# Sample rows of the expert layer summed on VectorE alone, and token rows spread over partitions by eight wide matmuls

## The chip, the cores and the metric

The kernel runs on one core of one Trainium2 chip. The metric is the device time of one execution in microseconds (us); a kernel's time is the median of its runs. PE (TensorE) does the matmuls, DVE (VectorE) and ACT (ScalarE) the elementwise work, POOL (GpSimd) issues gathers by index and some loads, SP (SyncE) issues the loads of the large tables.

## The reference

One inference step of a decoder with two layers, for 256 prompt tokens and 32 sample tokens of 1024 columns. Each layer ends in a mixture of 16384 experts, in which each token takes 8 x 16 = 128 experts by index:

```
def block(xb):
    ...
    top_s, pos = lax.top_k(cand, TOPK)
    expert = jnp.take_along_axis(cand_idx, pos, axis=-1)
    g = jax.nn.softmax(top_s, axis=-1).astype(xb.dtype)
    u = u_tab[expert]
    v = v_tab[expert]
    act = jax.nn.gelu(jnp.einsum('td,thkd->thk', xb, u), approximate=False)
    return jnp.einsum('thk,thkd->td', g * act, v)
```

The change is in how `xb` and the second einsum are brought about for the tokens whose `u` and `v` rows are gathered. All is float32.

## The kernel before

**The dense part.** 240 of the prompt tokens are done densely: both tables stream through the core, 128 tiles of 128 x 1024 each of `ut` and `vt` per layer, loaded on SP's queue. Each tile is split into a high part `wh` (ACT, L234) and a rest `wl` (DVE, L235). A `u` tile takes 24 matmuls of 240 columns (L463 to L465) into `pu`, and after every second one ACT stores its activation (L1340). A `v` tile takes 24 as well (`vmm`, L1317 to L1319) into `acc`; for every second one the stored activations, weighted meanwhile by the gates, are split into `gh` (ACT, L439) and `gl` (DVE, L440). This is the main stream.

**The gathered part.** The 16 prompt tokens that are left (`extra`, L1389) and the 32 sample tokens (`sample`, L1428) read their rows by index. A partition stands for a token and some of its heads, and one indirect DMA (`gather`, L1370, issued by POOL at L1372) brings one row of 1024 values for each of the 128 partitions into a tile `grow`: 16 such gathers from each table for `extra`, 32 for `sample`. In a first round DVE multiplies each gathered `u` row with the token's own row and sums it (L1410, L1455). The activation and the gate make of it one factor per partition and row (`act`, L1457 to L1460). In a second round the `v` rows are summed with these factors: `extra` does it on DVE into `saccx`, `sample` in two ways. The first `CPS[l]` rows, 8 in layer 0 and 4 in layer 1, are summed on TensorE: DVE makes `S2` (L1462), the product of all factors with the matrix `sel` that says which token a partition stands for, and two matmuls of 32 output columns per row (L1488) add up into a PSUM tile `so`, which ACT then copies out to `sacc[0]` (L1474). The rest is added up on DVE into `sacd`, one instruction per row (L1483 the first, L1481 the others). A gather is issued two rows ahead (`AH`); the tag `g4k` has 5 buffers in this part of the kernel, of which the two accumulators take one each and the rows three.

**What sets the order.** The main stream is written tile by tile. After each tile it calls `pump` (L1097), which lets generators in the background emit a step: those in `self.bg` by a budget of costs, and `self.bg2`, which is `extra` and then `sample`. While `v` tiles run and `self.bg` is empty, `bg2` makes one step per tile. A `yield` ends a step. Before the matmuls of L1488 `sample` sets `idle2` and waits until `self.bg` is nearly empty. Each engine works through its own list in the order of emission.

**Token rows.** For the products with the `u` rows each partition needs its token's row. `rows_in` (L1377) makes it from the transposed tokens `src`, which is 128 x 8 x 32: a matmul with the identity turns 128 x 32 columns around into 32 partitions of 128, and this is done four times for four groups of 32 partitions, 32 matmuls in all, into two PSUM tiles `hfp`, each copied by ACT to a half of `hft`. It is called once by `extra` and once by `sample` in each layer.

**The layer's end.** `peer_end` (L1493) first turns the sums back, with 24 matmuls into `pf`: for each of 8 column blocks one of `saccx`, one of `sacc[0]` and one of `sacd`, the last two added up in PSUM. VectorE's gates on `pf` follow.

## Time and profile before

| | us |
|---|---|
| median of 3 runs | 2097.3 (2096.06 to 2103.64) |
| profiled execution | 2090.24 |
| its span, first to last instruction | 2088.4 |
| PE busy in it | 1987.2 |
| DVE busy in it | 1690.8 |
| ACT busy in it | 915.4 |
| POOL busy in it | 360.5 |

The mean granted clock of TensorE is 0.985 of full speed. The busy shares are averages over the whole span, in which the stages differ, so the stages themselves are read from windows and timelines of the trace. Idle time of an engine is given with what ended it; "issue" there is time in which the engine waited for nothing that the profile shows. The main stream's pace can be read from the count of one of its lines in a stretch, 8 to a tile.

### The profile page before, as it was taken

Reading aid. Unit: us, or ns where it says so; the run is one execution under the profiler, and the core shown is the slowest. Engines: PE = TensorE matmul, PEld = TensorE weight load, DVE = VectorE, ACT = ScalarE, POOL = GpSimd, SP = SyncE. Lnnn points to the kernel's source line nnn. Section 1 sums busy time; section 2 is a strip of 40 time slices with the busy share of each in tenths; the row PEclk is TensorE's granted clock in tenths of the full one; section 3 lists DMA queues with packets and bytes.
Section 4 is the critical chain, followed back from the end, with each engine's and each line's share of the span. In section 5 each row is a group of like instructions: output and inputs, shape, how many; then the busy total and the mean of one; then the engine's idle time right before and its main releaser. Section 6 shows DMA issues by size and latency. Waiting matters only on the chain.

```text
span 2088.4 us, 46457 instructions
## 1 busy us (share of the span) xinstructions
PE 1987.2 (95%) x19170; PEld 1858.5 (89%) x19170; DVE 1690.8 (81%) x3392; ACT 915.4 (44%) x1215; POOL 360.5 (17%) x329
## 2 busy tenths in 40 slices
PE   7999999999999999999988889999999999999997
PEld 3777999999999999889966569999999999998997
DVE  3786898888889989777576478989888899887975
ACT  1855444444444444344341454444444444443443
POOL 1100001302211130253012200013031111302520
PEclk9999999999999999999999899999999999999998
DMA  9776456857867786799469734668578677956982
GB/s 366 256 258 225 129 184 192 311 173 247 297 210 251 244 300 218 263 330 339 141 193 258 271 130 131 191 198 305 166 268 279 222 240 244 318 171 227 339 303 72
DMA packets 135908, 493.88 MB, mean 236 GB/s; under 512 B 16032, under 2 KB 16544, under 8 KB 135056
## 3 DMA queue, kind: packets, MB, share of 16 engines
q1 hardware_dynamic: 93168, 334.09, 48.9%
q0 software_dynamic: 42528, 156.83, 21.2%
q8 instruction: 150, 2.46, 0.5%
q14 instruction: 62, 0.51, 0.1%
HBM read 483.41 MB, written 7.39 MB: 235 GB/s over the span
## 4 chain that ended last, share of the span: by engine, by line
PE 54%; issue 18%; DVE 12%; DMA 9%; POOL 4%; ACT 2%; SPq 0%; POOLq 0%; DVEq 0%; ACTq 0%
PE pu L465 7%; PE pu L463 7%; PE pu L464 7%; PE acc L1318 6%; PE acc L1317 6%; PE acc L1319 6%; DMA grow<-vt,ei 4%; POOL grow L1372 4%; DVE wl L235 3%; PE prj L463 2%; PE prj L465 2%; PE prj L464 2%; DMA R<-us 2%; PE adap L402 1%; PE pgt L1275 1%
## 5 line engine op out<-in xcount | busy, mean ns | idle before, releaser
L234 ACT CAST wh<-raw 128x1024 fp32r<-128x1024 f32 x583 | 610.6, 1049 | 609.5 <-PE acc L1318 327.7
L235 DVE TENSOR_TENSOR wl<-raw,wh 128x1024 fp32r<-128x1024 f32 x583 | 706.3, 1219 | 155.0 <-ACT wh L234 146.9
L465 PE MATMUL pu<-aH,wl 128*128 128x240 f32 x2048 | 566.0, 276 | 9.7 <-DVE wl L235 9.3
L1318 PE MATMUL acc<-gl,wh 128*128 128x240 f32 x2048 | 567.4, 277 | 6.3 <-DVE gl L440 6.2
L1317 PE MATMUL acc<-gh,wh 128*128 128x240 f32 x2048 | 570.1, 278 | 2.3 <-ACT gh L439 2.3
L463 PE MATMUL pu<-aH,wh 128*128 128x240 f32 x2048 | 567.3, 277 | 0.9 <-issue 0.7
L1319 PE MATMUL acc<-gh,wl 128*128 128x240 f32 x2048 | 566.5, 277 | 1.0 <-DVE wl L235 1.0
L464 PE MATMUL pu<-aL,wh 128*128 128x240 f32 x2048 | 563.6, 275 | 0.7 <-issue 0.7
L465 PEld LDWEIGHTS pu<-aH,wl 128*128 128x128 f32 x2048 | 389.5, 190 | 13.2 <-DVE wl L235 12.2
L1317 PEld LDWEIGHTS acc<-gh,wh 128*128 128x128 f32 x2048 | 391.0, 191 | 8.9 <-issue 4.6
L1318 PEld LDWEIGHTS acc<-gl,wh 128*128 128x128 f32 x2048 | 391.4, 191 | 8.5 <-DVE gl L440 8.3
L1319 PEld LDWEIGHTS acc<-gh,wl 128*128 128x128 f32 x2048 | 390.9, 191 | 1.7 <-DVE wl L235 1.6
L463 PEld LDWEIGHTS pu<-aH,wh 128*128 128x128 f32 x2048 | 388.5, 190 | 1.5 <-issue 1.3
L464 PEld LDWEIGHTS pu<-aL,wh 128*128 128x128 f32 x2048 | 388.8, 190 | 0.7 <-issue 0.7
L1340 ACT ACTIVATE store<-pu 128x480 f32<-128x480 f32 x128 | 73.2, 572 | 227.7 <-PE pu L465 227.6
L1372 POOL DMA_INDIRECT grow<-ur,ei x64 | 89.4, 1397 | 382.8 <-DVE grow L1455 275.2
L1372 POOL DMA_INDIRECT grow<-vt,ei x64 | 102.4, 1599 | 193.3 <-DVE grow L1455 113.2
L464 PE MATMUL prj<-aL,wh 128*128 128x288 f32 x392 | 116.3, 297 | 3.7 <-issue 3.7
L463 PE MATMUL prj<-aH,wh 128*128 128x288 f32 x392 | 119.6, 305 | 0.0
L1251 DVE TENSOR_TENSOR oA<-c,iT 128x1280 f16<-128x1280 f16 (+1 forms) x136 | 116.3, 855 | 0.0
L465 PE MATMUL prj<-aH,wl 128*128 128x288 f32 x392 | 116.1, 296 | 0.0
L1282 DVE SCALAR_TENSOR_TENSOR store<-pgt,store 128x460 f32<-128x460 f32 (+3 forms) x184 | 83.6, 499 | 33.2 <-PE pgt L1275 32.9
(366 smaller groups left out, 2681.4 us busy)
## 6 DMA issues: line engine op xcount, KB each, us to landing
raw<-ut SPq DMA_DIRECT2D x256, 512.0 KB
raw<-vt SPq DMA_DIRECT2D x256, 512.0 KB
adaw<-wada POOLq DMA_DIRECT2D x56, 512.0 KB
raw<-w SPq DMA_DIRECT2D x54, 512.0 KB
raw<-wq SPq DMA_DIRECT2D x32, 512.0 KB
adaw<-wada SPq DMA_DIRECT2D x18, 512.0 KB
R<-us POOLq DMA_DIRECT2D x32, 286.5 KB
store<-wada POOLq DMA_DIRECT2D x12, 512.0 KB
```

Source lines behind the costliest of these rows:

```text
L234: nc.scalar.copy(hf, r)
L235: nc.vector.tensor_sub(lf, r, hf.bitcast(F32))
L463: nc.tensor.matmul(pt, h[:, kb], ah[:, ka, n0:n1], start=f, stop=False)
L464: nc.tensor.matmul(pt, h[:, kb], al[:, ka, n0:n1], start=False, stop=False)
L465: nc.tensor.matmul(pt, lo[:, kb], ah[:, ka, n0:n1], start=False, stop=e)
L1251: v.tensor_tensor(a, self.iota2[:, None].to_broadcast([128, g, 128, 2]), bc(0, 128), op=ALU.is_equal)
L1282: v.scalar_tensor_tensor(sv, pg[:, :n, q0 - j0:q1 - j0].rearrange("p t j -> p j t"), 1.0 / 4096.0, sv, op0=ALU.mult, op1=ALU.mult)
L1317: nc.tensor.matmul(o, vh[:, d], wh, start=f, stop=False, skip_group_check=True)
L1318: nc.tensor.matmul(o, vh[:, d], wl, start=False, stop=False, skip_group_check=True)
L1319: nc.tensor.matmul(o, vl[:, d], wh, start=False, stop=e, skip_group_check=True)
L1340: nc.scalar.activation(store[:, s:s + 2], pu[:, :, :ND], AF.Gelu)
L1372: self.nc.gpsimd.indirect_dma_start(out=r, out_offset=None, in_=tab, in_offset=bass.IndirectOffsetOnAxis(ap=ei[:, w, c:c + 1], axis=0))
```

## The change

First, `sample` no longer uses TensorE for `v` rows. `CPS`, `S2`, the wait with `idle2`, the matmuls of L1488 and `sacc[0]` go; all 32 rows are added up on DVE into `sacd`, one per step. Second, `peer_end` has 16 matmuls in place of 24. Third, `rows_in` has ACT copy `src` four times side by side into `rep`, a buffer of the tag `g4k`, and eight matmuls of 128 columns take the place of 32 of 32 columns.

```diff
 def rows_in(self, src):
     nc, ps = self.nc, self.ps
+    rep = self.bp.tile([128, KT, 4, 32], F32, name="rep", tag="g4k", bufs=self.g4b)
+    nc.scalar.copy(rep, src[:, :, None, :].to_broadcast([128, KT, 4, 32]))
     hft = self.bp.tile([128, D], F32, name="hft", tag="g4k", bufs=self.g4b)
     for b in range(2):
         pt = ps.tile([128, 4, 128], F32, name="hfp", tag="g", bufs=2)
         for k in range(4):
-            for hg in range(4):
-                nc.tensor.matmul(pt[32 * hg:32 * hg + 32, k], src[:, 4 * b + k], self.ident,
-                                 start=True, stop=True, skip_group_check=True)
+            nc.tensor.matmul(pt[:, k], rep[:, 4 * b + k].rearrange("p a b -> p (a b)"), self.ident,
+                             start=True, stop=True, skip_group_check=True)
         nc.scalar.copy(hft[:, 512 * b:512 * b + 512], pt.rearrange("p a b -> p (a b)"))
...
 def sample(self, l, TKs):
...
     v.tensor_mul(act, act, g.rearrange("p h r -> p (h r)"))
-    S2 = self.bp.tile([128, 32, 32], F32, name="S2", tag="g4k", bufs=self.g4b)
-    v.tensor_mul(S2, act[:, :, None].to_broadcast([128, 32, 32]),
-                 self.sel[:, None, :].to_broadcast([128, 32, 32]))
-    yield 1200
-    self.idle2 = True
-    while len(self.bg) > 1:
-        yield 0
-    self.idle2 = False
-    po = ps.tile([128, 512], F32, name="so", tag="g", bufs=2)
+    yield 0
+    d = self.sacc = self.bp.tile([128, D], F32, name="sacd", tag="g4k", bufs=self.g4b)
     for c in range(32):
-        if c == CP:
-            self.sacc = [wp.tile([128, 512], F32, name="sacc", tag="sacc"),
-                         self.bp.tile([128, D], F32, name="sacd", tag="g4k", bufs=self.g4b)]
-            nc.scalar.copy(self.sacc[0], po)
         if c + AH < 32:
             gather(vrows, 1, c + AH)
         r = rows.pop((1, c))
-        if c >= CP:
-            d = self.sacc[1]
-            if c > CP:
-                v.scalar_tensor_tensor(d, r, act[:, c:c + 1], d, op0=ALU.mult, op1=ALU.add)
-            else:
-                v.tensor_scalar(d, r, act[:, c:c + 1], None, op0=ALU.mult)
-            yield 1200
-            continue
-        for i in range(2):
-            gq = 64 * (c % 2) + 32 * i
-            nc.tensor.matmul(po[gq:gq + 32], S2[:, c], r[:, 512 * i:512 * i + 512],
-                             start=c < 2, stop=c >= CP - 2, skip_group_check=True)
-        self.tp += 600
-        yield 0
+        if c:
+            v.scalar_tensor_tensor(d, r, act[:, c:c + 1], d, op0=ALU.mult, op1=ALU.add)
+        else:
+            v.tensor_scalar(d, r, act[:, c:c + 1], None, op0=ALU.mult)
+        yield 1200
...
 def peer_end(self, l):
...
-        nc.tensor.matmul(pf[:, k, XP:], self.sacc[0][:, 128 * (k % 4):128 * (k % 4) + 128],
-                         self.c32[:, 288 + 32 * (k // 4):320 + 32 * (k // 4)], start=True, stop=False,
-                         skip_group_check=True)
-        nc.tensor.matmul(pf[:, k, XP:], self.sacc[1][:, 128 * k:128 * k + 128], self.sel, start=False, stop=True,
+        nc.tensor.matmul(pf[:, k, XP:], self.sacc[:, 128 * k:128 * k + 128], self.sel, start=True, stop=True,
                          skip_group_check=True)
```

The lines after L99 move up by one in the changed kernel (L235 is L234 there). Three places show how the instructions stand.

VectorE in layer 0, where the round of `v` rows of the sample tokens begins; before, from the last step of the activation (L1460) on:

```order
L1460 TENSOR_TENSOR sact<-sact,gsel 128x32
L1462 TENSOR_TENSOR S_11427<-sact,c_68 128x1024
L235 TENSOR_TENSOR wl<-raw,wh 128x1024
L440 TENSOR_TENSOR gl<-store,gh 128x480
L235 TENSOR_TENSOR wl<-raw,wh 128x1024 x2
L440 TENSOR_TENSOR gl<-store,gh 128x480
L235 TENSOR_TENSOR wl<-raw,wh 128x1024 x2
L440 TENSOR_TENSOR gl<-store,gh 128x480
L1483 TENSOR_SCALAR sacd<-grow,sact 128x1024
L1481 SCALAR_TENSOR_TENSOR sacd<-grow,sact,sacd 128x1024
```

And in the changed kernel, from the same instruction on:

```order
L1459 TENSOR_TENSOR sact<-sact,gsel 128x32
L1469 TENSOR_SCALAR sacd<-grow,sact 128x1024
L234 TENSOR_TENSOR wl<-raw,wh 128x1024
L439 TENSOR_TENSOR gl<-store,gh 128x480
L1467 SCALAR_TENSOR_TENSOR sacd<-grow,sact,sacd 128x1024
L234 TENSOR_TENSOR wl<-raw,wh 128x1024
L1467 SCALAR_TENSOR_TENSOR sacd<-grow,sact,sacd 128x1024
L234 TENSOR_TENSOR wl<-raw,wh 128x1024
L439 TENSOR_TENSOR gl<-store,gh 128x480
L1467 SCALAR_TENSOR_TENSOR sacd<-grow,sact,sacd 128x1024
```

The instruction for `S2` is gone, and `sacd` begins one place after the activation instead of after eight instructions of the main stream; from there one accumulation stands in each tile until all 32 are done.

ScalarE at the first call of `rows_in` in layer 0, before:

```order
L1340 ACTIVATE store<-pu 128x480
L234 CAST wh<-raw 128x1024 x2
L1340 ACTIVATE store<-pu 128x480
L1386 COPY hft<-hfp 128x512 x2
L234 CAST wh<-raw 128x1024 x2
```

And in the changed kernel:

```order
L1339 ACTIVATE store<-pu 128x480
L233 CAST wh<-raw 128x1024 x2
L1339 ACTIVATE store<-pu 128x480
L1379 COPY rep<-hfx 128x1024
L1386 COPY hft<-hfp 128x512 x2
L233 CAST wh<-raw 128x1024 x2
```

The copy to `rep` stands behind the activation `store<-pu` of the tile just ended and before the two copies of `hfp`.

TensorE at the same call, before:

```order
L464 MATMUL pu<-aL,wh 128x240
L465 MATMUL pu<-aH,wl 128x240
L1384 MATMUL hfp<-c_68,hfx 32x128 x32
L463 MATMUL pu<-aH,wh 128x240
L464 MATMUL pu<-aL,wh 128x240
L465 MATMUL pu<-aH,wl 128x240
L463 MATMUL pu<-aH,wh 128x240
```

And in the changed kernel:

```order
L463 MATMUL pu<-aL,wh 128x240
L464 MATMUL pu<-aH,wl 128x240
L1384 MATMUL hfp<-c_68,rep 128x128 x8
L462 MATMUL pu<-aH,wh 128x240
L463 MATMUL pu<-aL,wh 128x240
L464 MATMUL pu<-aH,wl 128x240
L462 MATMUL pu<-aH,wh 128x240
```

The place in the main stream is the same; 32 matmuls that read `hfx` became 8 that read `rep`. On POOL the order of the gathers is the same in both kernels; six loads of `wada` that stand among the layer 0 gathers of `vt` come a few gathers earlier or later. In the changed kernel the last accumulation of `sample` stands four tiles later in layer 0 and two in layer 1.

## Rows read from the trace of the kernel before

**Rows 1.** The page's busy time of each engine (busy us, share of the span, instructions), its costliest groups of instructions for ScalarE and VectorE, and of the groups by line on VectorE two more; in a group's line stand the busy time, the mean ns of one, and the idle time before them with what ended it.

```profile
PE 1987.2 (95%) x19170; PEld 1858.5 (89%) x19170; DVE 1690.8 (81%) x3392; ACT 915.4 (44%) x1215; POOL 360.5 (17%) x329
L234 ACT CAST wh<-raw 128x1024 fp32r<-128x1024 f32 x583 | 610.6, 1049 | 609.5 <-PE acc L1318 327.7
L235 DVE TENSOR_TENSOR wl<-raw,wh 128x1024 fp32r<-128x1024 f32 x583 | 706.3, 1219 | 155.0 <-ACT wh L234 146.9
...
L440 DVE TENSOR_TENSOR gl<-store,gh 128x480 fp32r<-128x480 f32 x128 | 83.2, 650 | 0.0
L1481 DVE SCALAR_TENSOR_TENSOR sacd<-grow,sact,sacd 128x1024 f32<-128x1024 f32 x50 | 64.1, 1282 | 21.6 <-DMA grow<-vt,ei 20.7 <-DVE gl L440 0.3
```

**Rows 2.** Busy time in six stretches of the instructions of L1317 alone, the first of three matmuls of a `v` block (8 of them in a tile): the stretch in us, its length, PE busy (count), PEld busy (count), granted clock, DMA share, GB/s. The first three stretches lie in layer 0, the last three in layer 1.

```profile
876.93:897.88 20.95, 6.92 (x24) 4.55 (x24) 1.00 0.89 324
897.88:963.75 65.87, 49.52 (x177) 34.26 (x177) 0.97 0.97 363
980.00:1020.00 40.00, 32.63 (x120) 22.45 (x120) 1.00 0.70 213
1917.57:1927.55 9.98, 2.32 (x8) 1.52 (x8) 0.91 0.92 333
1927.55:2008.17 80.62, 62.36 (x225) 43.02 (x225) 0.99 0.96 348
2020.00:2056.00 36.00, 29.36 (x108) 20.22 (x108) 1.00 0.51 160
```

**Rows 3.** The same view of the first stretch of each layer, of the instructions of L1488 alone (the matmuls that sum sample rows).

```profile
876.93:897.88 20.95, 7.88 (x32) 1.15 (x32) 1.00 0.89 324
1917.57:1927.55 9.98, 4.59 (x16) 0.62 (x16) 0.91 0.92 333
```

**Rows 4.** The timeline of VectorE around the first and the last of the accumulations of sample rows in each layer: start us, duration us, engine, line, operation, out<-in, and in brackets the idle time before it with what ended it.

```profile
898.74 0.97 DVE L1483 TENSOR_SCALAR sacd<-grow,sact 128x1024 f32<-128x1024 f32 x1 [1.79 <-DMA grow<-vt,ei]
903.39 1.28 DVE L1481 SCALAR_TENSOR_TENSOR sacd<-grow,sact,sacd 128x1024 f32<-128x1024 f32 x1 [3.68 <-DMA grow<-vt,ei]
...
969.73 1.29 DVE L1481 SCALAR_TENSOR_TENSOR sacd<-grow,sact,sacd 128x1024 f32<-128x1024 f32 x1 [0.80 <-DMA grow<-vt,ei]
...
1927.67 0.75 DVE L1483 TENSOR_SCALAR sacd<-grow,sact 128x1024 f32<-128x1024 f32 x1 [2.71 <-PE so L1488]
1931.66 1.28 DVE L1481 SCALAR_TENSOR_TENSOR sacd<-grow,sact,sacd 128x1024 f32<-128x1024 f32 x1 [3.24 <-DMA grow<-vt,ei]
...
2008.03 1.28 DVE L1481 SCALAR_TENSOR_TENSOR sacd<-grow,sact,sacd 128x1024 f32<-128x1024 f32 x1
```

**Rows 5.** The timeline of GpSimd around the first gathers of `vt` rows of the sample tokens, four in layer 0 and the first of layer 1; columns as in rows 4.

```profile
869.29 1.71 POOL L1372 DMA_INDIRECT grow<-vt,ei  x1 [20.07 <-DVE grow L1455]
...
904.95 1.67 POOL L1372 DMA_INDIRECT grow<-vt,ei  x1 [4.04 <-DVE sacd L1481]
907.31 1.68 POOL L1372 DMA_INDIRECT grow<-vt,ei  x1 [0.69 <-DVE sacd L1481]
910.21 1.68 POOL L1372 DMA_INDIRECT grow<-vt,ei  x1 [1.22 <-DVE sacd L1481]
...
1909.93 1.68 POOL L1372 DMA_INDIRECT grow<-vt,ei  x1 [92.54 <-DVE grow L1455]
```

**Rows 6.** The view of one tile, `S` (which takes in `S2`): operation and count, duration of one in ns (least, median, greatest), first and last start in us.

```profile
L1462 DVE TENSOR_TENSOR S<-sact,c x2: 1225/1225/1225, 874.3 to 1914.9; 128x1024 f32<-128x1024 f32 x2
```

**Rows 7.** Busy time of each engine in a stretch of layer 0 in which row gathers and their products run beside the tiles: the stretch, its length, PE, PEld, DVE, ACT and POOL busy (count), granted clock, DMA share, GB/s.

```profile
520.00:540.00 20.00, 20.00 (x180) 20.00 (x179) 19.03 (x18) 9.24 (x11) 11.01 (x7) 1.00 1.01 394
```

**Rows 8.** The same view of the transposing back at the end of each layer, of the tile `pf` alone (PE, PEld and DVE busy).

```profile
1023.35:1029.38 6.03, 6.03 (x48) 5.89 (x48) 0.00 (x0) 0.89 0.61 183
2056.63:2061.91 5.28, 5.28 (x48) 5.28 (x48) 0.00 (x0) 1.00 0.01 3
```

**Rows 9.** The timeline of TensorE at the third call of `rows_in` (layer 1), the rows of `hfp`; columns as in rows 4, two records for one matmul of this shape.

```profile
1402.09 1.72 PE L1384 MATMUL hfp<-c,hfx 128*32 128x128 f32 x51
...
1403.99 0.44 PE L1384 MATMUL hfp<-c,hfx 128*32 128x128 f32 x5 [0.19 <-issue]
1404.73 0.44 PE L1384 MATMUL hfp<-c,hfx 128*32 128x128 f32 x6 [0.30 <-issue]
1405.49 0.38 PE L1384 MATMUL hfp<-c,hfx 128*32 128x128 f32 x2 [0.31 <-issue]
```

**Rows 10.** Busy time of the instructions of the tile `pu` (the main matmuls of a `u` tile) in four stretches, each from the start of a call of `rows_in`: PE, PEld and ACT busy (count). A matmul that already runs at the start of a stretch is counted in it.

```profile
361.62:371.34 9.72, 6.69 (x52) 6.13 (x51) 1.10 (x2) 1.00 0.83 286
1402.09:1416.22 14.13, 9.56 (x81) 9.24 (x81) 1.14 (x2) 1.00 0.84 287
595.12:598.69 3.57, 0.07 (x1) 0.00 (x0) 0.57 (x1) 1.00 0.95 291
1635.27:1638.83 3.56, 0.07 (x1) 0.00 (x0) 0.57 (x1) 1.00 0.78 260
```

**Rows 11.** The timelines of ScalarE and, in the last row, of VectorE at the first and the third call of `rows_in`; columns as in rows 4.

```profile
361.73 0.57 ACT L1340 ACTIVATE store<-pu 128x480 f32<-128x480 f32 x1 [1.75 <-PE pu L465]
...
368.29 0.59 ACT L1386 COPY hft<-hfp 128x512 f32<-128x512 f32 x1 [4.62 <-PE pu L465]
...
1408.62 0.58 ACT L1386 COPY hft<-hfp 128x512 f32<-128x512 f32 x1 [2.52 <-remote]
...
368.91 1.23 DVE L1410 SCALAR_TENSOR_TENSOR grow<-grow,hft 128x1024 f32<-128x1024 f32 x1 [6.68 <-ACT hft L1386]
```

More of the change, by code (lines that the diff above doesn't have):

```diff
@@ L98 @@
 BG4 = 1
-CPS = (8, 4)
 J1 = 46
@@ L1116, in pump @@
                 self.step2()
-                if self.bg2 is None or self.idle2:
+                if self.bg2 is None:
                     break
@@ L1228, in peer @@
         xtra = self.extra(l)
-        self.von = self.idle2 = False
+        self.von = False
         self.bg += [tk_sample(), fin(0), fin(1)]
@@ L1444, in sample @@
         rows = {}
-        CP = CPS[l]
         gather = self.gatherer(ei, rows)
```

## The prediction

> **What bounds the kernel now.** I read the page's busy shares first [rows 1]: TensorE is busy for 95% of the span, VectorE for 81%. So a VectorE instruction costs nothing by itself; it costs what it makes TensorE wait. The question for each stretch is how long TensorE takes per weight tile there. A tile of the second table (`v`) is 24 matmuls, 8 of them on L1317, so the count of L1317 in a window divided by 8 is the number of tiles done [rows 2]. Undisturbed, 40.00 us hold 120, and 36.00 us hold 108: 15 tiles and 13.5, both 2.667 us per tile. That is the floor that I measure everything against.
>
> The same rows show the stage that is changed, in layer 0 and in layer 1. While TensorE sums sample rows, 20.95 us hold 24 (3 tiles) and 9.98 us hold 8 (1 tile): 8.0 and 2.67 us of main work, so 12.95 and 7.31 us are lost to it. The group of the row matmuls [rows 3] has only 7.88 and 4.59 us of work in these stretches; the rest is TensorE standing still behind a matmul that waits for its gathered row, with the main matmuls queued behind it. Then VectorE sums the other rows: 65.87 us hold 177 (22.1 tiles, 2.98 us each), 80.62 us hold 225 (28.1 tiles, 2.87 us each). So a row on VectorE costs TensorE about 0.31 us in layer 0 and 0.20 us in layer 1, a row on TensorE 1.62 and 1.83 us.
>
> **Why a VectorE row costs anything.** Each tile needs one `wl` (1219 ns) and half a `gl` (650 ns), and the row adds 1282 ns [rows 1]: 2.83 us by these durations, slightly less as they follow each other with overlap, against 2.667 us of TensorE. VectorE is at its limit, and each wait of the row for its gather goes to `wl` behind it and on to TensorE. The rows themselves follow each other by (969.73 - 898.74) / 23 = 3.09 us in layer 0 and (2008.03 - 1927.67) / 27 = 2.98 us in layer 1 [rows 4]; a gather starts when VectorE has given a buffer back (904.95, 907.31, 910.21 [rows 5]).
>
> **Part 1: 12 more rows on VectorE, none on TensorE.** The order shows one row per tile from the tile after the activation, 32 tiles in a row. I compare 32 tiles from the start of the TensorE rows. Layer 0 before: 20.95 + 65.87 + (32 - 25.1) x 2.667 = 105.2 us; after, 32 x 2.98 = 95.4. Layer 1 before: 9.98 + 80.62 + (32 - 29.1) x 2.667 = 98.3; after, 32 x 2.87 = 91.8. The gain is 9.8 + 6.5 = **16.3 us**. The tile before the stage also loses the product for `S2` (1225 ns [rows 6]), whose cover was VectorE's slack, and ScalarE one copy; I cost them at nothing. Rows now end 4 tiles later in layer 0 and 2 in layer 1, with 17 tiles or more still to come, so the end isn't late. On the POOL queue six loads for the next layer's conditioning stand among the gathers, before as after; they are moved by a few gathers and have no one waiting near.
> Bounds: if rows dictate the pace at 3.09 and 2.98 us, the 32 tiles take 98.9 and 95.4, and the gain is 6.3 + 2.9 = 9.2. If the pace were the floor, 85.3 each, it is 19.9 + 13.0 = 32.9; a stretch with such rows and TensorE at full count does exist, 180 matmuls in 20 us at 394 GB/s [rows 7]. I take the pace that this stage itself showed, since there `gl` comes in every second tile.
>
> **Part 2: the transposing back at the layer's end.** Of 24 matmuls 8 go. The block takes 6.03 us in layer 0 and 5.28 in layer 1 [rows 8], TensorE does nothing else in it and VectorE waits for its end. A third of each: 2.0 + 1.8 = **3.8 us**. Bounds: 1.8 each, or 2.7 in all if the first write to a bank has a fixed part; 4.5 if VectorE's wait falls with it.
>
> **Part 3: spreading the token rows, four times.** Before: 32 small matmuls whose spread to 4 column groups lets them run together: 51 records, two for a matmul, in 1.72 us [rows 9]. But the burst doesn't end so. TensorE then issues in drops of 5 or 6 records, and what it loses is more than the array time. In the first call, 9.72 us hold 51 main matmuls, in the third (layer 1) 14.13 us hold 80 [rows 10]; at 0.111 us each (40.00 us / 360) 4.0 and 5.2 us are lost; in the second and fourth nothing but the burst is in 3.57 and 3.56 us. Together 16.4 us. In the first and third ScalarE gets its second half only at 368.29 and 1408.62, and VectorE stands for 6.68 us before the first row [rows 11].
> After: ScalarE makes a copy of 1024 columns first, and eight full matmuls wait for it. The copy stands behind the activation that itself waits for the matmuls just ahead, so nothing covers it: 0.57 us of activation, about 1.05 us for the copy (a cast of the same size takes 1049 ns [rows 1]), some 0.15 us of hand-over, then 8 x 0.22 us (5.28 / 24 [rows 8]) = 1.76. That is 3.53 us, four times 14.1 us: a gain of **2.3 us**, if 32 instructions in place of 128 go out without drops. VectorE's stand of 6.68 us should fall to about 3.7.
> Bounds: nothing hides the wait and the drops were an accident of the profile: the wait alone is added, 4 x 1.77 = 7.1 us lost. The wait is covered after all: 16.4 - 7.0 = 9.4 gained.
> The rows show four small matmuls in the time of about one large one: 51 records in 1.72 us are 67 ns a matmul, 0.27 us for four, against 0.22. The Trainium skill ("TensorE: Matmul & The Clock Gate", section "Part 3: Packing small matmuls — row/col tiling") has the same as a rule: matmuls on different column groups run in the array at once, so four narrow ones cost little more than one. By that rule alone the eight wide ones save no array time, this part loses 7.1 us for its copy, and the whole sum would be 13.0 instead of 22.4. The trace agrees with the rule on the burst and not on what comes after it.
>
> **Sum.** 16.3 + 3.8 + 2.3 = 22.4 us. The profiled execution took 2090.24 us, span 2088.4 and 1.8 around it; that becomes 2067.8. The median of the runs is 2097.3, 7.1 above; I carry the difference over: 2097.3 - 22.4 = **2074.9**. A measurement of this kernel can tell about 0.5%, 10.5 us, from no change.
>
> **Rivals.** (a) *Transfers bound the stage.* In the changed stretches the DMA engines are busy for 0.89, 0.97, 0.92 and 0.96 of the time [rows 2]. Four and two more tiles must be loaded in the same stage; if they fit only in the time left free, the gain of part 1 is 20.95 x 0.11 + 65.87 x 0.03 + 9.98 x 0.08 + 80.62 x 0.04 = 8.3 us, the sum 14.4, the time 2082.9. For it: 363 GB/s already. Against it: 394 GB/s seen [rows 7], and 32 rows, 32 tiles and 6 loads of 0.524 MB in 95.4 us are 385 GB/s, layer 1 without the loads 366.
> (b) *No change.* Part 1 at its low bound (9.2) and part 3 at its loss (7.1): 9.2 + 3.8 - 7.1 = 5.9, the time 2091.4.
> (c) *Slower: the gather's wait moves into VectorE's queue at its start.* The first rows now come while the gathers have just begun: the first started at 869.29 and 1909.93 us, and in the present kernel the first accumulations wait 3.68 and 3.24 us [rows 4, 5], with `wl` and the main stream behind. If such waits came at every third row, because three buffers go round, the pace would be 2.667 + 3.4 / 3 = 3.8 us, 32 tiles 121.6 us: 16.4 and 23.3 lost, less 6.1 elsewhere: 33.6 slower, 2130.9. It decides from a pace of 3.27 us on, where the sum is zero (203.5 us before, plus 6.1, over 64 tiles is 3.27). Against it: 24 and 28 rows in a chain already run at 2.98 and 2.87 with the same three buffers.
> (d) That the change isn't made: excluded, the order shows 32 accumulations in a layer and 8 matmuls for 32.
>
> **How the numbers follow.** The forecast 0.62, (a) 0.17, (b) 0.14, (c) 0.07. The forecast's own range goes from 2063 (part 1 about 8 better than its pace, part 3 a few better) to 2085. (a) lies in it, (b) reaches to 2091.4; leaving out (c) and the far ends gives **2062 to 2091**. Faster by over 0.5% (under 2086.8): the forecast and (a), 0.79, less a little for their edges, 0.78; same: 0.15; slower: 0.07.
>
> **What would show it.** Right: no stretch where TensorE does 3 tiles in 20 us; L1317's successor at 8 per 2.9 us over 32 tiles; a dip of the granted clock (0.91 in the 9.98 us) gone; the block at the layer's end at 4.0 and 3.5 us; after each copy a TensorE wait of 1.6 to 1.9 us and then 16 records without gaps. Wrong: rows 3.3 us apart with VectorE waiting for gathers; waits for `wl` in place of the matmuls' waits; drops after the eight matmuls as before.

## The result, and the profile after

The changed kernel takes 2072.1 us (median of 4 runs, 2067.63 to 2073.99) against 2096.7 (2093.36 to 2103.64): a ratio of 0.9879, with an interval of 0.9853 to 0.9904, that is 1.2% faster. Its profiled execution took 2067.63 us, span 2065.8, 22.6 us less than the one before. The forecast was 2074.9, with 22.4 us gained, in a range from 2062 to 2091. The time was right, in part by luck: the runs below show that two of the three terms of the sum were not, and that for the largest, whose size was about right, the reason given was not.

First the page and the groups by line, to be held against [rows 1]:

```profile
PE 1962.2 (95%) x18898; PEld 1844.5 (89%) x18898; DVE 1702.2 (82%) x3402; ACT 919.3 (44%) x1217; POOL 367.6 (18%) x329
L234 DVE TENSOR_TENSOR wl<-raw,wh 128x1024 fp32r<-128x1024 f32 x583 | 707.7, 1222 | 126.5 <-ACT wh L233 121.4
...
L1467 DVE SCALAR_TENSOR_TENSOR sacd<-grow,sact,sacd 128x1024 f32<-128x1024 f32 x62 | 79.5, 1283 | 24.9 <-DMA grow<-vt,ei 24.5
```

VectorE has 11 us more to do and waits less for `wh` (121 us in place of 147). The stage is best read in windows that run from the start of the same tile to the start of another. Here of the kernel before and then of the changed one, the main matmuls of one line alone (PE and PEld busy with counts, granted clock, DMA share, GB/s): 33 tiles of layer 0 and 38 of layer 1 that hold all the `v` rows of the sample tokens, and two of the last three `v` tiles with the transposing back between them, in layer 0 and in layer 1.

```profile
874.13:982.94 108.81, 73.76 (x265) 50.75 (x265) 0.98 0.94 350
1906.61:2021.61 115.00, 84.29 (x305) 58.09 (x305) 0.99 0.92 330
1020.67:1034.44 13.77, 5.65 (x16) 4.27 (x17) 0.77 0.39 119
2053.95:2066.30 12.35, 5.24 (x16) 3.85 (x17) 0.86 0.01 1
```

```profile
878.76:980.90 102.14, 72.62 (x265) 50.04 (x265) 1.00 0.96 366
1894.43:2002.37 107.94, 83.64 (x304) 57.65 (x305) 1.00 0.96 349
1018.63:1027.59 8.96, 4.49 (x16) 3.04 (x17) 1.00 0.56 186
2034.71:2043.67 8.96, 4.49 (x16) 3.04 (x17) 1.00 0.01 2
```

The stage went from 108.81 to 102.14 and from 115.00 to 107.94 us. What it would be without rows is in the changed kernel's 14 tiles just behind it, 2.695 us each:

```profile
980.90:1018.63 37.73, 30.76 (x112) 21.20 (x113) 1.00 0.70 219
```

So 33 tiles have a floor of 88.9 and 38 one of 102.4, and the changed kernel is still 13.2 and 5.5 us above it. The layer's end went from 13.77 to 8.96 and from 12.35 to 8.96, more than the block itself, whose two windows of the tile `pf` answer to [rows 8]:

```profile
1021.32:1024.81 3.49, 3.49 (x32) 3.49 (x32) 0.00 (x0) 1.00 0.53 174
2037.50:2041.00 3.50, 3.50 (x32) 3.44 (x31) 0.00 (x0) 1.00 0.02 5
```

The rest is the clock. The tile that follows the block in layer 0, before and after (same columns as above):

```profile
1029.19:1034.44 5.25, 3.45 (x8) 2.79 (x9) 0.50 0.01 4
```

```profile
1024.81:1027.59 2.78, 2.29 (x8) 1.59 (x9) 1.00 0.52 183
```

Before, TensorE had the lower of its two levels there (0.50, 1.2 GHz in place of 2.4) after 24 matmuls of 16 and 32 columns in a row; the same work took 5.25 us in place of 2.78. After 16 such matmuls it kept 2.4 GHz in this trace, in both layers.

The first and the last accumulation of sample rows in each layer (timeline of VectorE, to be held against [rows 4]):

```profile
879.07 0.76 DVE L1469 TENSOR_SCALAR sacd<-grow,sact 128x1024 f32<-128x1024 f32 x1 [0.18 <-DMA grow<-vt,ei]
...
977.94 1.28 DVE L1467 SCALAR_TENSOR_TENSOR sacd<-grow,sact,sacd 128x1024 f32<-128x1024 f32 x1
...
1902.98 0.97 DVE L1469 TENSOR_SCALAR sacd<-grow,sact 128x1024 f32<-128x1024 f32 x1 [0.26 <-DMA grow<-vt,ei]
...
1994.03 1.28 DVE L1467 SCALAR_TENSOR_TENSOR sacd<-grow,sact,sacd 128x1024 f32<-128x1024 f32 x1
```

They begin without the waits of 3.68 and 3.24 us that the first ones had, and run (977.94 - 879.07) / 31 = 3.19 and (1994.03 - 1902.98) / 31 = 2.94 us apart.

At the first call of `rows_in`, ScalarE, TensorE and VectorE in the changed kernel (timelines; to be held against [rows 9, 11]):

```profile
362.90 0.57 ACT L1339 ACTIVATE store<-pu 128x480 f32<-128x480 f32 x1 [1.75 <-PE pu L464]
363.37 1.04 ACT L1379 COPY rep<-hfx 128x1024 f32<-128x1024 f32 x1
```

```profile
364.46 2.05 PE L1384 MATMUL hfp<-c,rep 128*128 128x128 f32 x16 [1.59 <-ACT rep L1379]
```

```profile
370.05 1.23 DVE L1410 SCALAR_TENSOR_TENSOR grow<-grow,hft 128x1024 f32<-128x1024 f32 x1 [6.43 <-DMA grow<-ur,xi]
```

TensorE waits 1.59 us for the copy, and its 16 records go out without drops: that is as forecast, in all four calls. But VectorE waits 6.43 us as before (6.68), now for the first gathered row instead of for `hft` (5.72 us in the third call).

### The profile page after: what moved, and what is told of

It reads as the page before. It is cut to its first block, busy times and chain, and to the rows that moved or that the text cites. A ratio compares the mean times of both kernels' runs of the same rounds, so it can differ in the third digit from the quotient of the medians.

```text
span 2065.8 us, 45941 instructions
## 1 busy us (share of the span) xinstructions
PE 1962.2 (95%) x18898; PEld 1844.5 (89%) x18898; DVE 1702.2 (82%) x3402; ACT 919.3 (44%) x1217; POOL 367.6 (18%) x329
## 4 chain that ended last, share of the span: by engine, by line
PE 54%; issue 18%; DVE 13%; DMA 8%; POOL 4%; ACT 3%; DVEq 0%; SPq 0%; POOLq 0%; ACTq 0%
PE acc L1317 7%; PE acc L1316 7%; PE acc L1318 7%; PE pu L464 5%; PE pu L462 5%; PE pu L463 5%; DMA grow<-vt,ei 4%; POOL grow L1371 4%; DVE wl L234 3%; PE prj L462 2%; PE prj L464 2%; PE prj L463 2%; PE adap L401 1%; DMA R<-us 1%; PE pd L881 1%
## 5 line engine op out<-in xcount | busy, mean ns | idle before, releaser
L234 DVE TENSOR_TENSOR wl<-raw,wh 128x1024 fp32r<-128x1024 f32 x583 | 707.7, 1222 | 126.5 <-ACT wh L233 121.4
L1317 PE MATMUL acc<-gl,wh 128*128 128x240 f32 x2048 | 566.3, 277 | 9.5 <-DVE gl L439 9.2
L1316 PE MATMUL acc<-gh,wh 128*128 128x240 f32 x2048 | 566.9, 277 | 2.3 <-ACT gh L438 2.3
L462 PE MATMUL pu<-aH,wh 128*128 128x240 f32 x2048 | 566.5, 277 | 0.0
L463 PE MATMUL pu<-aL,wh 128*128 128x240 f32 x2048 | 562.9, 275 | 0.0
L1317 PEld LDWEIGHTS acc<-gl,wh 128*128 128x128 f32 x2048 | 388.9, 190 | 13.6 <-DVE gl L439 12.9
L464 PEld LDWEIGHTS pu<-aH,wl 128*128 128x128 f32 x2048 | 389.1, 190 | 12.2 <-DVE wl L234 12.0
L1316 PEld LDWEIGHTS acc<-gh,wh 128*128 128x128 f32 x2048 | 388.5, 190 | 2.7 <-ACT gh L438 2.7
L463 PEld LDWEIGHTS pu<-aL,wh 128*128 128x128 f32 x2048 | 388.0, 189 | 0.0
L462 PEld LDWEIGHTS pu<-aH,wh 128*128 128x128 f32 x2048 | 387.1, 189 | 0.4 <-issue 0.4
L1371 POOL DMA_INDIRECT grow<-ur,ei x64 | 89.4, 1397 | 382.5 <-DVE grow L1454 268.7
L1371 POOL DMA_INDIRECT grow<-vt,ei x64 | 109.0, 1703 | 189.2 <-DVE grow L1454 111.9
L462 PE MATMUL prj<-aH,wh 128*128 128x288 f32 x392 | 119.5, 305 | 0.0
L463 PE MATMUL prj<-aL,wh 128*128 128x288 f32 x392 | 116.1, 296 | 0.0
```

Of the source, the lines that this page charges most:

```text
L234: nc.vector.tensor_sub(lf, r, hf.bitcast(F32))
L462: nc.tensor.matmul(pt, h[:, kb], ah[:, ka, n0:n1], start=f, stop=False)
L463: nc.tensor.matmul(pt, h[:, kb], al[:, ka, n0:n1], start=False, stop=False)
L464: nc.tensor.matmul(pt, lo[:, kb], ah[:, ka, n0:n1], start=False, stop=e)
L1316: nc.tensor.matmul(o, vh[:, d], wh, start=f, stop=False, skip_group_check=True)
L1317: nc.tensor.matmul(o, vh[:, d], wl, start=False, stop=False, skip_group_check=True)
```

## The experiments

Times are medians; a ratio is to the kernel before on the same chip. "Stage" means the windows above, 33 tiles of layer 0 and 38 of layer 1; "end" the windows of the last tiles.

| run | us (before) | ratio, interval | stage 0 | stage 1 | end 0 | end 1 |
|---|---|---|---|---|---|---|
| kernel before | 2096.7 | | 108.8 | 115.0 | 13.8 | 12.4 |
| changed | 2072.1 (2096.7) | 0.9879, 0.9853 to 0.9904 | 102.1 | 107.9 | 9.0 | 9.0 |
| e1 | 2098.5 (2095.3) | 1.0020, 1.0002 to 1.0038 | 114.7 | 113.3 | 12.4 | 14.0 |
| e2 | 2078.5 (2095.3) | 0.9929, 0.9902 to 0.9956 | 101.7 | 109.9 | 9.0 | 10.6 |
| e3 | 2074.3 (2095.3) | 0.9904, 0.9876 to 0.9931 | 100.4 | 108.8 | 12.4 | 14.0 |
| e4 | 2070.8 (2095.3) | 0.9889, 0.9864 to 0.9913 | 103.7 | 109.1 | 10.6 | 9.0 |
| e5 | 2053.8 (2094.6) | 0.9804, 0.9779 to 0.9830 | 89.0 | 102.5 | 9.0 | 10.5 |
| e6 | one run, 2056.4 | | 89.0 | 102.5 | 10.6 | 10.6 |
| e7 | one run, 2064.9 | | 97.8 | 107.4 | 12.2 | 12.0 |
| e8 | 2107.6 (2094.6) | 1.0075, 1.0046 to 1.0104 | 120.5 | 118.0 | 15.3 | 14.0 |
| e10 | 2044.8 (2093.2) | 0.9752, 0.9729 to 0.9774 | 89.4 | 102.5 | 10.6 | 12.0 |
| e11 | one run, 2055.9 | | 91.4 | 102.5 | 10.5 | 11.8 |
| e12 | 2041.6 (2093.2) | 0.9738, 0.9712 to 0.9764 | 91.3 | 102.5 | 9.0 | 9.0 |
| e13 | 2036.8 (2089.8) | 0.9734, 0.9708 to 0.9761 | 89.0 | 102.5 | 9.0 | 9.0 |

**e1: part 3 alone.** The kernel before with the new `rows_in`.

> The kernel before with part 3 alone: the copy to rep and eight wide matmuls in each of the four calls, sample rows and layer's end as before. My theory from the two traces: a call costs TensorE 1.59 us of waiting for the copy and 1.81 us for the matmuls, 3.40 us where the old burst took 3.57 in the second and fourth call, so those gain 0.2 each; in the first and third call the old loss is replaced by the wait for the first gathered row behind which wl stands, so they gain 0 to 1. Together 0 to 2.5 us faster than the kernel before, not to be told from it. Rival one, the prediction's part 3 as written: 2.3 faster. Rival two, the narrow matmuls were free and the copy is pure loss: 7.1 us slower.

It is 0.2% slower, with an interval of 0.4 to 8 us that just leaves out no change, and with it my theory and rival one; rival two's 7.1 us lie in it. But the calls themselves show no loss: 12 tiles around the first took 38.7 us in place of 38.5, around the third 37.8 in place of 38.7, and four around the second and the fourth 15.4 in place of 15.5. Its profiled execution took 2090.31 us, as long as the one before (2090.24); layer 0's stage, which the edit doesn't touch, is 5.9 us longer in it, and other places are shorter. So the traces have no place for a loss of 7 us in the calls, and none for a gain; the medians alone don't exclude the loss.

**e2: parts 1 and 2 alone.** The changed kernel with the old `rows_in`.

> The changed kernel with the old way of spreading token rows (32 narrow matmuls, no copy): parts 1 and 2 without part 3. My theory: nearly the whole gain stays, 22 to 25 us faster than the kernel before. Rival (the copy loses 7.1 us in the changed kernel): 31 us faster than the kernel before, that is 7 faster than the changed one.

The ratio gives 15 us of gain (9 to 21), less than my theory and the rival had. That would leave part 3 some 10 in the changed kernel, where e1 has a small loss for it. The two don't add up, and the traces have no place for either: the first call cost 1.5 us more in the changed kernel's profile, the third 0.8 less. It is not only the occasion: e3 and e4, measured beside e2, have the new `rows_in` and are 4 and 8 us faster than e2 by the medians. In the windows of the calls part 3 is about nothing; what it is worth in the medians stays open.

**e3: part 2 undone.** A third tile is turned back beside the two sums:

```diff
+        self.s0 = wp.tile([128, 4, 128], F32, name="sacc", tag="sacc")
+        nc.scalar.mul(self.s0, self.ones[:, None, :].to_broadcast([128, 4, 128]), 0.0)
...
+            nc.tensor.matmul(pf[:, k, XP:], self.s0[:, k % 4], ..., start=True, stop=False, ...)
-            nc.tensor.matmul(pf[:, k, XP:], self.sacc[:, 128 * k:128 * k + 128], self.sel, start=True, stop=True,
+            nc.tensor.matmul(pf[:, k, XP:], self.sacc[:, 128 * k:128 * k + 128], self.sel, start=False, stop=True,
```

> The changed kernel with 24 matmuls at the layer's end again: a third tile that holds zeros is turned back beside the two sums, so part 2 alone is undone. Theory A (the block of small matmuls and the waits around it bring TensorE to its lower clock, which the tile behind then pays for): 6 to 9 us slower than the changed kernel, that is 16 to 19 faster than the kernel before, and the granted clock at 0.5 in or right behind the block in one or both layers, with the last two tiles 5 us in place of 2.8. Rival (only the block's own length counts): 2.3 + 1.8 = 3.5 to 4.5 us slower than the changed kernel, clock 1.00 at both blocks.

The ends of the two layers, in the window of the changed kernel's 8.96 us:

```profile
1015.63:1027.98 12.35, 5.18 (x16) 3.82 (x17) 0.86 0.41 135
2040.76:2054.74 13.98, 5.66 (x16) 4.25 (x17) 0.76 0.00 1
```

Both are back at 12 to 14 us, with clocks of 0.86 and 0.76. At full clock they would be 12.35 x 0.86 and 13.98 x 0.76, 10.6 us each: 1.7 us are the block's length and the rest is the clock. Theory A holds in the trace, where the two ends are 8.4 us longer than the changed kernel's; the medians (21 us faster than before, 15 to 26) can't tell it from the changed kernel's 25 (20 to 31). Over all kernels here the end took 13.5 us on average with 24 matmuls (8 layer ends, a fall of the clock at each) and 10.1 with 16 (20 ends, a fall at 11 of them). TensorE stands still at none of these 28 ends, so of theory A's two reasons the block is left and the waits around it are not. So the 16 matmuls make a fall rarer and don't exclude it; that the changed kernel's profile has none at either end is partly chance.

**e4: the copy earlier.** `rep` is made when `bg2` is set up, for `sample` before its `yield 400`; `rep_in` holds the two lines that made it:

```diff
+                self.repx = self.rep_in(self.hfx)
                 self.bg2 = chain(xtra, smp)
...
+        rep = self.rep_in(self.hfs)
         yield 400
-        hft = self.rows_in(self.hfs)
+        hft = self.rows_in(rep)
```

> The changed kernel with rep copied earlier: for the extra tokens two tiles earlier, for the sample tokens one tile earlier; all else the same. Theory A (in the first and third call the first gathered row is late anyway, VectorE and the wl behind it wait for it, so only the second and fourth call gain): 2 x 1.59 = 3.2 us faster than the changed kernel. Rival B (TensorE's wait for the copy is lost time in each call): 4 x 1.59 = 6.4 us faster. Rival C (something else holds TensorE at these places): no gain.

What the instructions of `hfp` waited for (us, times, PE and PEld together), in the changed kernel and then in e4:

```profile
  ACT rep L1379: 13.5, 8
```

```profile
  PE hfp L1388: 2.5, 8
```

The second is the only wait left there, ScalarE's for the matmuls: TensorE's wait for the copy is gone in all four calls. The 12 tiles around the first and the third call took 40.4 and 38.3 us, 40.2 and 37.9 in the changed kernel: no gain there. For the second and fourth call the 3.2 us are too small for the medians, but the traces show them: the four tiles around each took 13.56 us in place of 15.43, 1.9 less twice. So theory A holds in the traces, and rivals B and C fall.

**e5: two rows in three tiles.**

```diff
+            self.td = max(self.td, self.tp)
             yield 1200
+            while self.pn % 3 == 2:
+                self.td = max(self.td, self.tp)
+                yield 0
```

> The changed kernel with the 32 rows of the sample tokens accumulated in two of three tiles instead of in each, over 47 tiles instead of 32; work and transfers are the same. In the changed kernel the stage of rows costs TensorE 0.43 us per tile above its floor in layer 0 (102.1 us for 33 tiles from the 79th v tile on, floor 88.0) and 0.17 us in layer 1 (107.9 us for 38 tiles, floor 101.3). Theory A (VectorE has no slack in a tile with a row, 2.83 us against 2.667, so every wait for a gather reaches TensorE): with 2.40 us of VectorE work per tile the waits are covered and most of the 14.1 + 6.6 us comes back, 12 to 20 us faster than the changed kernel. Rival B (transfers bound the stage): the same bytes over 47 tiles in place of 32, so some 10 us come back in layer 0 and little in layer 1. Rival C (each row's wait for its gather reaches TensorE whatever VectorE's load): no gain, within 3 us.

```profile
880.68:969.63 88.95, 72.52 (x264) 49.96 (x265) 1.00 0.98 368
1889.95:1992.45 102.50, 83.59 (x304) 57.63 (x305) 1.00 0.90 323
```

The stage is at its floor in both layers (L1316 alone), with 33 and 38 tiles in 88.95 and 102.50 us, and the kernel is 41 us faster than the one before. The rows now run on past these windows, and the tiles behind lose nothing either: the 14 behind layer 0's window took 37.73 us, as in the changed kernel. Rival C falls. Whether VectorE or the transfers got the room, the next two tell.

**e6: half the gathers, all of VectorE's work.** Every second gather is left out and each row used twice.

> The changed kernel with every second gather of vt rows for the sample tokens left out: each gathered row is accumulated twice, with two factors, so half of the sum's rows are wrong. VectorE's work is unchanged, the stage's gathers are halved. Theory A (VectorE is at its limit and the gathers' waits come on top): the pace falls to VectorE's own 2.83 us, 33 tiles of layer 0 in 93 to 95 us where the changed kernel has 102.1, 38 tiles of layer 1 in 105 to 107 where it has 107.9. Rival B (transfers bound): both fall to the floor, 88 to 89 and 101 to 102 us. Rival C (VectorE's work alone sets it): no change, within 1 us of 102.1 and 107.9.

Busy time of all engines in the two stages (PE, PEld, DVE, ACT, POOL), and in the second fence all that VectorE waited for these gathers in layer 0 (us, times, longest):

```profile
878.27:967.22 88.95, 88.95 (x795) 88.95 (x793) 85.77 (x84) 43.11 (x50) 25.94 (x20) 1.00 0.92 333
1887.74:1990.24 102.50, 102.50 (x920) 102.50 (x916) 97.52 (x98) 48.57 (x57) 27.37 (x17) 1.00 0.81 289
```

```profile
DVE sacd L1470 <- DMA grow<-vt,ei: 0.2, 1, 0.2
```

With one full row per tile and VectorE busy for 85.77 of 88.95 us, TensorE is at its floor. Theory A's VectorE at its limit falls: it needs 2.60 us per tile (85.77 / 33) of 2.695. The changed kernel's own stage in layer 0 says the same, with as much VectorE work in a longer time:

```profile
878.76:980.90 102.14, 92.98 (x795) 90.09 (x793) 85.47 (x83) 43.09 (x50) 55.83 (x37) 1.00 0.96 366
```

What B forecast came.

**e7: all gathers, hardly any work on VectorE.**

```diff
-                v.scalar_tensor_tensor(d, r, act[:, c:c + 1], d, op0=ALU.mult, op1=ALU.add)
+                v.scalar_tensor_tensor(d[:, :64], r[:, :64], act[:, c:c + 1], d[:, :64], op0=ALU.mult, op1=ALU.add)
```

> The changed kernel with the accumulations of the sample tokens' vt rows made on 64 of 1024 columns only, so most of the sum is left out; all gathers are issued and waited for. Theory A (a full VectorE passes the gathers' waits on): VectorE has 1.1 us of slack in each tile and takes the waits up, 33 tiles of layer 0 in 88 to 92 us, 38 of layer 1 in 101 to 103. Rival B (transfers bound): no change in layer 0, 100 to 104 us. Rival C (waits for gathers reach TensorE whatever VectorE's load): 96 to 102 us in layer 0.

```profile
877.29:975.13 97.84, 91.80 (x795) 89.72 (x794) 56.40 (x84) 43.04 (x50) 49.89 (x37) 1.00 0.98 379
1889.99:1997.36 107.37, 104.76 (x918) 104.35 (x915) 67.25 (x97) 48.53 (x57) 50.10 (x33) 0.98 0.95 349
```

VectorE is down to 56.40 us and the stage still takes 97.84, 8.9 above its floor: the row's wait reaches TensorE with an idle VectorE too, since `wl` stands behind it. Theory A falls, and C's forecast came; B's low end is missed by 2 us. The rows come about every 3 us (97.84 / 32 = 3.06), and the median time of such a gather from issue to landing, in e7 and then in e5, is

```profile
grow<-vt,ei POOLq DMA_INDIRECT x64, 8.0
```

```profile
grow<-vt,ei POOLq DMA_INDIRECT x64, 6.8
```

8.0 us and three buffers make 2.7 us per row, before the wait for VectorE and for the next issue. The changed kernel's trace doesn't mark the landings, but it has the whole round: in layer 0 the median from a gather's issue to the start of its row's accumulation is 7.7 us, the accumulation takes 1.28, and 0.27 later the next gather into that buffer is issued. That is 9.25 us for three buffers, 3.08 per row, where rows were 3.19 apart; in layer 1 it is 7.1 us, and 2.88 against 2.94.

**e8: twice as many rows on TensorE in the kernel before**, `CPS = (16, 8)`.

> The kernel before with twice as many sample rows summed on TensorE, 16 in layer 0 and 8 in layer 1. Theory A (each row on TensorE costs 1.6 to 1.8 us, one on VectorE 0.2 to 0.3): 8 x 1.31 + 4 x 1.63 = 17 us slower than the kernel before. Rival (what the TensorE rows cost is their start, the first gathers' landing, so more rows cost little more than their 0.5 us of matmuls): 0 to 5 us slower.

```profile
875.90:996.35 120.45, 74.21 (x264) 50.77 (x265) 0.99 0.87 317
1917.87:2035.82 117.95, 84.08 (x305) 57.66 (x305) 1.00 0.89 322
```

It is 0.75% slower (0.46 to 1.04), 16 us, with 11.6 us more in layer 0's stage and 3.0 in layer 1's: 1.45 and 0.74 per row. The profile of e1, which has the same stage, is 5.9 longer and 1.7 shorter there than the one before; against the mean of the two it is 8.7 and 3.8 us, 1.1 and 0.9 per row. The rival falls by the medians; theory A holds for the total, and its split between the layers isn't shown.

This kernel's `rows_in` is that of the kernel before, and yet its 32 narrow matmuls go out without drops, in all four calls. TensorE at the second call:

```profile
596.87 1.96 PE L1384 MATMUL hfp<-c,hfs 128*32 128x128 f32 x64
```

From the burst's start to the next main matmul it is 1.88 us here and 3.57 in the kernel before. So the drops don't come with these 32 matmuls alone; what in a program brings them on stays open.

**e11: the same gathers with half the bytes.**

> The changed kernel with the 32 gathers of vt rows of the sample tokens bringing 512 columns per partition instead of 1024, from other rows of the table, each accumulated into both halves, so that most of the sum is wrong: as many gathers, as many and as long instructions on VectorE, half the bytes. Theory B (bytes: with a tile and a row per 2.667 us the DMA engines would have to move 393 GB/s, about the 394 that any stretch shows): 33 tiles of layer 0 in 88.9 to 91 us, 38 of layer 1 in 102.5 to 104, where the changed kernel has 102.1 and 107.9. Theory D (the round trip: three buffers, and each gather takes some 8 us to land plus its wait for a buffer, however many bytes): 97 to 102 and 105 to 108, no change.

```profile
876.26:967.70 91.44, 72.57 (x265) 50.00 (x265) 1.00 0.90 318
1885.78:1988.28 102.50, 83.59 (x304) 57.63 (x305) 1.00 0.85 288
```

**e12: the same bytes with a gather more in flight.** `g4b = 6` and, in `sample`, `AH = 3`.

> The changed kernel with six buffers of the tag g4k instead of five and the gathers of the sample tokens issued three rows ahead instead of two; the bytes are the same. Theory D (round trip of a gather through three buffers): with four in flight the stage comes to its floor, 89 to 92 us for the 33 tiles of layer 0 and 102.5 to 104 for the 38 of layer 1, 12 to 20 us faster than the changed kernel. Theory B (bytes): the gathers take longer to land and the stage stays within 3 us of 102.1 and 107.9.

```profile
873.42:964.73 91.31, 72.61 (x265) 50.04 (x265) 1.00 1.02 405
1881.18:1983.68 102.50, 83.66 (x305) 57.70 (x305) 1.00 0.96 366
```

Both bring the stage nearly or wholly to its floor, each against one theory. e12 decides against B: with all bytes, at 405 GB/s in place of 366, layer 0's stage is 2.4 us above its floor instead of 13.2. So the DMA engines had room left in the changed kernel. The Trainium skill ("Perfetto Trace Analysis", section "Roofline") puts what one core's DMA engines move together at about 435 GB/s; the 405 measured here lie below, so the trace agrees. e11 corrects D in one word: not "however many bytes". That half of them shorten the round trip is the likely reason, but no landing is marked in its trace. In e12 the round is longer, 10.1 us from issue to accumulation in layer 0 in place of 7.7, but four buffers share it: with 1.28 and 0.27 that is 2.9 us per row, and rows were 2.85 apart. VectorE's wait for these gathers in layer 0's stage (us, times, longest), in the changed kernel and in e12:

```profile
DVE sacd L1467 <- DMA grow<-vt,ei: 16.2, 15, 2.7
```

```profile
DVE sacd L1467 <- DMA grow<-vt,ei: 6.3, 6, 1.3
```

The gain over the changed kernel is some 30 us by the ratios, more than the 12 to 20 that theory D gave. The trace has 16.3 us of it in the two stages. Some of the rest is where `u` rows are gathered, through the same buffers: in 16 of layer 0's 256 tiles (the 161st on) VectorE waits 1.5 us for them in place of 6.8, and these tiles take 44.4 us in place of 47.4; the 12 tiles at the first call take 37.0 in place of 40.2 (38.2 to 40.8 in the kernels that have neither this edit nor e10's).

**e10: early copies, two rows in three tiles, and first products two tiles later** (in `extra`, before the loop over `u` rows):

```diff
-        yield 0
+        n = self.pn + 2
+        while self.pn < n:
+            self.td = max(self.td, self.tp)
+            yield 0
```

> The changed kernel with three things: the early copies of rep, the rows of the sample tokens accumulated in two of three tiles, and in the first and third call of rows_in the first product with a gathered row written two tiles later, behind two more wl. Theory A (in those calls VectorE waits about 6 us for the first gathered row, and wl and TensorE behind it): beyond the two-in-three kernel 3 to 4 us from the second and fourth copy, and 3 to 4 us in each of the first and third call (12 tiles from the 34th u tile on in 34 to 36 us where the changed kernel has 40.2 and 37.9); 43 to 52 us faster than the kernel before. Rival B (what TensorE loses after the first and third call has another cause, such as the gathers' transfers holding up the tile loads): those 12 tiles stay at 37.5 us or more, 41 to 45 us faster than the kernel before.

The 12 tiles around the first and the third call, in the changed kernel (L462) and in e10 (L463):

```profile
357.31:397.50 40.19, 26.46 (x96) 18.10 (x97) 1.00 0.90 314
1386.59:1424.44 37.85, 26.48 (x96) 18.00 (x97) 1.00 0.91 337
```

```profile
359.34:398.09 38.75, 27.14 (x97) 18.92 (x96) 0.96 0.92 331
1376.86:1412.25 35.39, 26.45 (x97) 18.18 (x96) 1.00 0.95 346
```

The third came to 35.4 us as theory A had it; the first to 38.75, of which a fall of the clock to 0.96 has 1.6, so 37.1: 3 us less than in the changed kernel, which is in the 3 to 4 expected, but not in the 34 to 36. The total (48 us by the medians, 52 by the ratio) is that of theory A.

**e13: e10 with the buffers of e12.**

> The last kernel but one of these runs (early copies, rows in two of three tiles, first products two tiles later) with the six buffers and three gathers ahead of the run before. Theory D (the rows' cost was the round trip of the gathers, and both remedies take away the same wait): the stage of rows stays at its floor, 88.9 to 89.5 and 102.5 us, and what is gained over either kernel comes from the other's part alone: 1.8 in the third call over the three-ahead kernel, 1.6 for each early copy in the second and fourth call and 2.4 in layer 0's stage; together 2 to 7 us faster than the three-ahead kernel, 53 to 60 faster than the kernel before. Rival (the buffers gain something of their own at other places): over 60 faster than the kernel before.

It is the fastest of these kernels: 2036.8 us, 53 faster than the kernel before by the medians, and 35 below the median that the changed kernel had on another occasion. Its interval overlaps that of e12, and in its profile the parts add as theory D says: the stage at 88.95 and 102.50, the 12 tiles at the first and third call at 35.1 and 35.3 us, 1.9 less than e12 each.

## Why the prediction was right, and where it was not

**The sum** was 22.4 and the profile shows 22.6, because one term was too small by about what the two others were too large. That is luck.

**Part 1, 16.3 forecast.** From the mean stages of the kernels with TensorE rows (before, e1: 111.8 and 114.1) and without, else as the changed kernel (changed, e2, e3, e4: 102.0 and 108.9) it is 9.8 + 5.2 = 15.0; in the two profiles alone, 6.7 + 7.1 = 13.7. The size was about right; the step "VectorE is at its limit" was not. It rested on adding single durations, 2.83 us against a floor taken as 2.667 (windows that don't begin with a tile count a few matmuls too many); e6 has 2.60 per tile against 2.695. The row's cost was its gather's round trip through three buffers, with `wl` queued behind the wait (e6, e7, e12 agree on it). That part of the section, "each wait of the row for its gather goes to `wl` behind it", was the whole of it. That a row on TensorE costs more than one on VectorE was right (e8).

**Part 2, 3.8 forecast.** The block shrank by 4.3 us (to 3.49 and 3.50), about what was said, yet the end gained 8.2 us in the two profiles and 6.8 on average (2 x 3.4). The term was mis-sized by the clock: the rows showed 0.89 in the block, and the prediction left out the tile behind it. How much of the 8.2 a single execution gets is chance, since the fall also comes after 16 matmuls.

**Part 3, 2.3 forecast.** About 0 in the windows of the calls; the medians of e1 and e2 don't settle it. The burst costs 1.59 + 1.81 = 3.40 us in place of 3.57 in the second and fourth call, close to the 3.53 forecast (no row shows its 0.15 us of hand-over; from the copy's end to the first matmul it was 0.05). The step that failed is "VectorE's stand of 6.68 us should fall to about 3.7": it was 6.43 and 5.72, since the landing of the first gather was next, and the prediction left out what else that row waits for. The 3.57 us that were to be saved were less firm than they seemed as well: in e8 the same burst took 1.88, against which the copy would lose 1.5 us in each of these two calls.

**Rivals.** (a) falls with e12: the same bytes, at 405 GB/s. (b), no change, rested on a low bound for part 1 that did not come. (c) had the mechanism that the runs show, waits of VectorE because three buffers go round, but made it too large: VectorE waited 16.2 us for these gathers in layer 0's stage, hardly at its start (0.18 us), and rows were 3.19 us apart in layer 0 and 2.94 in layer 1, below the 3.27 from which it decides, in layer 0 not by much.

## What to carry to other kernels

When a stream of gathers feeds an engine that works in order beside a main stream, count the round trip of one gather divided by its buffers before blaming the engine or the bandwidth: one buffer more, with gathers issued one row further ahead, was worth about as much as the whole change. Test the cause with work halved and gathers halved apart; a sum that comes out right does not say that its terms were. And read the granted clock of the tiles behind a block of small matmuls, not only of the block.

## What the runs showed of the hardware that was not expected

The transposing back pulled TensorE down from 2.4 to 1.2 GHz for part of the tiles behind it at each of 8 layer ends with 24 matmuls of 16 and 32 columns, and at 11 of 20 with 16 such matmuls; the tile behind took 4.1 to 5.25 us in place of 2.78 where it fell. TensorE had no wait at any of these ends. A gather of 128 rows of 4 KB took 8.0 us from issue to landing with a row about every 3 us (e7), and 6.8 us with one every 4 (e5); the main loads ran on beside them at up to 405 GB/s in all without slowing TensorE by more than 2.4 us in 33 tiles. The same 32 narrow matmuls took 3.57 us in one program, with gaps of 0.2 to 0.3 us in which TensorE waited for nothing that the profile shows, and 1.88 us without gaps in another with the same source for them (e8).
